# Spreading two norms' inverse roots with two 512-column float32r products each

## The chip, the core and the metric

One core of one Trainium2 chip runs the whole program in one launch. The metric is the device time of an execution in microseconds (us). Three runs of the kernel before took 697.29, 698.58 and 698.46 us; their median is 698.46.

## The reference

A decoder block over 512 positions of width 1024, in fp32:

```python
h  = rmsnorm(x, norm1_g)                       # x * rsqrt(mean(x^2) + eps) * g
P  = h @ w_in                                  # mixer A, q/k/v of mixer B, branch gates, two merge gates
yA = B * causal_dwconv3(C * x_in)
yB = nsa(q, compressed / selected / window keys, gates)
x  = x + W_o(sigmoid(gA) * (yA @ W_A) + sigmoid(gB) * (yB @ W_B))
h  = rmsnorm(x, norm2_g)
x  = x + W_down(silu(causal_dwconv3(W_g h) + b) * (W_u h))   # FFN, inner width 2816

def rmsnorm(x, g):
    x32 = x.astype(jnp.float32)
    y = x32 * lax.rsqrt(jnp.mean(x32 * x32, axis=-1, keepdims=True) + EPS)
    return (y * g.astype(jnp.float32)).astype(x.dtype)
```

Each norm has one inverse root per position, 512 of them.

## The kernel before

Activations are held with channels on the partitions and the 512 positions along the columns. Every large product is made in float32r out of a rounded part and a rest: for a weight tile (wh, wl) and an activation tile (xh, xl), the helper `dense` issues wh·xh, wh·xl and wl·xh (L434, L435, L437), all into one accumulator. Rounded parts are written by ScalarE (ACT), rests by VectorE (DVE), or by a DMA that adds the source to the negated rounded part (L170 to L172).

The norms are not applied to the activations ahead of the products. A product runs on x times its gain, and the inverse root of each position is multiplied in after it. For this the inverse roots, which come out as a 128x4 tile `r` (position on the partition), are needed as a 128x512 tile `rb`: the 512 values along the columns, the same on every partition. `row_scales` makes it: TensorE (PE) sums the squares over the partitions (L400), DVE turns them into means (`ms`, L403), GpSimd (POOL) takes them to the power −0.5 (`r`, L391), PE spreads `r` over the partitions into a PSUM bank `pr`, and ACT copies that to `rb` (L419). The spreading of the first norm (n1) multiplies a tile of ones by the diagonal matrices `dg` (identity times r, made by DVE at L409) in four fp32 products of 128 columns (L412). That of the second (n2) multiplies r, broadcast along the columns, by the identity, in four fp32 products too (L416).

The first norm falls into the token projections (`pj` banks, products at L266 to L268 of `xg_h`, `xg_l` with weights `wh_t`, `wl_t` or `whx`, `wlx`). Its readers are the compressed keys (`kcb`, L469) and later the merge gates. The second falls between the output projection and the FFN.

The FFN works on pairs of 128 inner channels, eleven rounds, by seven products of half-width blocks per pair and matrix (`ff_pair`). The weight forms are `th`/`tl` (one block), `wh_s`/`wl_s` (two blocks, straight from the weights) and `sh`/`sl` (sums of blocks); the activation forms are `xf_h`, `xf_l`; a product has 256 columns. Sums are gathered by DVE in `c` (L1016, L1047), multiplied by `rb`, convolved, put through silu, and multiplied by the second matrix's result. The down projection (`pdn` banks, activations `ah`, `al`, weights `wh_d`, `wl_d`) is worked off between rounds. For the first pair, the first three quarters of the products (L1028) run before the last output projection, to cover the second norm.

Two things set the order of the work. Each engine runs its instructions in one fixed order that a scheduler lays down by simulating the program when it is built. And tiles come from pools: a tile with the same tag as an earlier one waits for that one's last reader. Pools are stacked in SBUF from two sides. On the left lie `sb` (constants, `r`, `rb`), then `pxg` (xg_h, later x1), then `pa` (xg_l, y0, y1, weights of the projections), and after `pa` is closed `px` (xf_h, xf_l) and `pw` (th, tl, sh, sl). On the right lie `pb`, `pp` (with the tag "w4" and whx, wlx), the ring `wf` (its wh and wl serve wh_bo, wh_o, wh_s, wh_d and others) and `pf` (ah, al, c0, c1, cv). Small tiles named `gap_x`, `gap_w` and so on pad the left stack.

Of the kernel before, what the change touches and what calls it, by code (L numbers as in the profile page):

```python
# [11 lines left out]
F32 = mybir.dt.float32  # L12
F32R = mybir.dt.float32r
I32 = mybir.dt.int32
AF = mybir.ActivationFunctionType
ALU = mybir.AluOpType
AX = mybir.AxisListType

P = 128
D = 1024  # L20
S = 512
KD = D // P
NT = S // P
# [19 lines left out]
TOKC = C_G + 24  # L43
NW4 = 4
# [41 lines left out]
def tile_block(ctx: ExitStack, tc: tile.TileContext, xT, pos, par, par2, w_tok, w_a3, w_gate, w_ao, w_bo, w_o,  # L86
               w_ff, w_dn, c_w1, out):
    nc = tc.nc
    sb = ctx.enter_context(tc.tile_pool(name="sb", bufs=1, side="left"))
# [8 lines left out]
    pp = pr_ctx.enter_context(tc.tile_pool(name="pp", bufs=1, side="right"))  # L98

    def const(shape, name, dt=F32, pool=sb):  # L100
        return pool.tile(shape, dt, name=name, tag=name)

    def w_tmp(name, shape):

        t = pp.tile([P, TOKC], F32, name=name, tag="w4", bufs=NW4)
        v = t[:, :math.prod(shape)]
        if len(shape) == 2:
            v = v.rearrange("p (a b) -> p a b", a=shape[0])
        elif len(shape) == 3:
            v = v.rearrange("p (a b c) -> p a b c", a=shape[0], b=shape[1])  # L110
        return v
# [77 lines left out]
    ones = const([P, P], "ones")  # L189
# [90 lines left out]
    sq_sum, first_d = [], []  # L280
# [95 lines left out]
    ident = const([P, P], "ident")  # L376
# [12 lines left out]
    def rsqrt(dst, src, n):  # L389

        nc.gpsimd.tensor_tensor(dst, src, mhalf[:, :n], op=ALU.pow)  # L391
# [3 lines left out]
    def row_scales(total, name, bank_of, dg):  # L395

        pr = bank_of(f"pr_{name}")
        for t in range(NT):
            for i, v in enumerate(total):
                sums = nc.tensor.matmul(pr[:, 2 * t:2 * t + 2], v[:, t * P:(t + 1) * P], ones[:, 0:2],  # L400
                                        start=i == 0, stop=i == len(total) - 1)
        ms = sb.tile([P, NT], F32, name=f"ms_{name}", tag="ms")
        nc.vector.tensor_scalar(ms, pr[:, 0:2 * NT].rearrange("p (t two) -> p t two", two=2)[:, :, 0], 1.0 / D, EPS,  # L403
                                op0=ALU.mult, op1=ALU.add)
        means[name] = ms
        r = sb.tile([P, NT], F32, name=f"r_{name}", tag=f"r_{name}")
        rsqrt(r, ms, NT)
        if dg is not None:
            nc.vector.tensor_tensor(dg, ident[:, None, :].to_broadcast([P, NT, P]), r[:, :, None].to_broadcast([P, NT, P]),  # L409
                                    op=ALU.mult)  # L410
            for t in range(NT):
                rows = nc.tensor.matmul(pr[:, t * P:(t + 1) * P], ones, dg[:, t, :], start=True, stop=True)  # L412
        else:
            for t in range(NT):

                rows = nc.tensor.matmul(pr[:, t * P:(t + 1) * P], r[:, t:t + 1].to_broadcast([P, P]), ident, start=True,  # L416
                                        stop=True)
        rb = sb.tile([P, S], F32, name=f"rb_{name}", tag="rb")
        nc.scalar.activation(rb, pr, AF.Copy)  # L419
        return r, rb, (sums, rows)  # L420

    r1, r1b, _ = row_scales((sq_sum[0][:, 0],), "n1", d_bank, w_tmp("dg_n1", (NT, P)))

    eps1 = const([P, NT], "eps1", F32, pp)
    nc.vector.tensor_scalar(eps1, means["n1"], EPS, None, op0=ALU.mult)
# [25 lines left out]
    for g in range(G):  # L451
        rows = slice((1 - g) * HD, (2 - g) * HD)
# [449 lines left out]
    sq2 = sb.tile([P, S], F32, name="sq2", tag="rb")  # L902
    for n, j in enumerate(O_ORDER):
# [18 lines left out]
        nc.scalar.activation(sq, xj, AF.Square)  # L922
        if n > 0:
            nc.vector.tensor_add(sq2, sq2, sq)
    _, r2b, (sums2, rows2) = row_scales((sq2,), "n2", d_bank, None)
    mx_ctx.close()


    pf = ctx.enter_context(tc.tile_pool(name="pf", bufs=1, side="right"))
# [9 lines left out]

    def pair_tile(name, tag):  # L940
        return pf.tile([P, 2, S], F32, name=name, tag=tag, bufs=1)

    u_bufs = []
    for i in range(NU):
# [106 lines left out]
    def ff_strassen(f, between):  # L1051
        u = u_bufs[f // 2 % NU]

        with tc.high_priority(offset=AHEAD if f == 0 else 0):
            form = ff_forms(f, 0)
        ff_pair(f, 0, u[:, :, 2:], form, late=f == 0 or None)
        between()
        nc.vector.tensor_tensor(u[:, :, 2:], u[:, :, 2:], r2two, op=ALU.mult)
        cv = pair_tile(f"cv{f}", "cv")
        for m in range(2):  # L1060
            conv_silu(f + m, cv[:, m], u[:, m])
        nc.vector.tensor_tensor(cv, cv, r2two, op=ALU.mult)
        up = pair_tile(f"up{f}", "up")
        ff_pair(f, 1, up, ff_forms(f, 1))

        between()
        nc.vector.tensor_tensor(up, up, cv, op=ALU.mult)
        for m in range(2):
            h, l = a_tiles(f + m)
            split(h, l, up[:, m])  # L1070
# [108 lines left out]
```

## Time and profile before

| | |
|---|---|
| runs | 697.29, 698.58, 698.46 us (median 698.46) |
| profiled execution: time, span | 699.54 us, 697.8 us |
| busy: PE, DVE, ACT, POOL | 690.3, 509.2, 436.7, 245.1 us |
| granted TensorE clock | 1.0 (2.4 GHz) over the whole span |
| the spreading of n1, of n2 | starts at 34.31 us, at 373.82 us |
| FFN products of xf with wh_s, wl_s | 363.4 to 660.5 us |

The span goes from the first to the last record of the profiled execution, and all times in the rows count from its start; the execution's own time holds what lies around the span too. A row of a timeline gives the start, the duration, engine, line, operation, tiles and shapes. A matmul's duration contains its whole way through the array and overlaps with the next, so what a product costs is read from one start to the next. An fp32 product leaves two records. A row of the chain of waits gives when a piece began to set the end, for how long, and what it was.

### The profile page before, as it was taken

The numbers are of one execution on the slowest core, as the hardware profiler recorded it, in microseconds if no ns is written. First come the engines' busy times: TensorE is split into PE (matmuls) and PEld (weight loads), VectorE is DVE, ScalarE is ACT, GpSimd is POOL, SyncE is SP. The second block draws the span as 40 slices with busy tenths as digits, with TensorE's granted clock in tenths as the row PEclk, the third lists the DMA queues.
The fourth block names the chain that finished last, engine by engine and source line by source line (L and its number), as shares of the span: only waits on it lengthen the run. The fifth ranks groups of instructions, "written<-read, shape, count | busy, mean of one in ns | idle before, by whom it ended". The sixth has DMA issues, their size and how long they took to land.

```text
span 697.8 us, 11271 instructions
## 1 busy us (share of the span) xinstructions
PE 690.3 (99%) x4123; PEld 615.4 (88%) x4123; DVE 509.2 (73%) x890; ACT 436.7 (63%) x776; POOL 245.1 (35%) x240
## 2 busy tenths in 40 slices
PE   9999999999999999999999999999999999999997
PEld 8999878878888887888889999999999999999986
DVE  6987975766576646376887999888787777877544
ACT  7635754768898877534776776666466665556530
POOL 4151432467888867552012221211112221112110
PEclk9999999999999999999999999999999999999999
DMA  7333686576776555573587977978977979875665
GB/s 264 116 97 121 159 185 142 143 249 203 250 225 214 172 175 151 179 244 100 141 194 169 234 179 190 224 178 200 221 173 173 213 179 213 184 175 108 133 138 151
DMA packets 56615, 124.87 MB, mean 179 GB/s; under 512 B 5232, under 2 KB 20976, under 8 KB 56560
## 3 DMA queue, kind: packets, MB, share of 16 engines
q1 hardware_dynamic: 35648, 79.39, 35.2%
q0 software_dynamic: 13840, 32.51, 27.4%
q10 hardware_dynamic: 7072, 12.26, 5.7%
q8 instruction: 32, 0.52, 0.3%
q14 instruction: 23, 0.19, 0.1%
HBM read 111.55 MB, written 12.58 MB: 178 GB/s over the span
## 4 chain that ended last, share of the span: by engine, by line
PE 87%; DMA 6%; ACT 2%; POOL 2%; issue 1%; DVE 1%; SPq 0%; POOLq 0%; ACTq 0%
PE p L435 10%; PE p L434 10%; PE p L437 10%; PE pdn L435 6%; PE pdn L434 6%; PE pdn L437 6%; PE pg L434 3%; PE pg L435 3%; PE pg L437 3%; DMA tn_e<-td_e 2%; PE po L435 2%; PE po L434 2%; PE po L437 2%; DMA wl_a<-in_w_a_dram 2%; PE pa L437 2%; PE pa L434 2%
## 5 line engine op out<-in xcount | busy, mean ns | idle before, releaser
L434 PE MATMUL p<-xf_h,sh 128*128 128x256 f32 x336 | 80.9, 276 | 0.0
L435 PE MATMUL p<-xf_l,sh 128*128 128x256 f32 x336 | 80.8, 276 | 0.0
L172 POOL DMA_DIRECT2D wl_s<-in_w_ff_dram x22 | 19.4, 883 | 165.4 <-ACT wl_s L171 151.5
L435 PE MATMUL pdn<-al,wh_d 128*128 128x512 f32 (+1 forms) x176 | 68.5, 389 | 0.0
L434 PE MATMUL pdn<-ah,wh_d 128*128 128x512 f32 (+1 forms) x176 | 68.2, 389 | 0.0
L164 ACT ACTIVATE sh<-s 128x1024 fp32r<-128x1024 f32 x44 | 46.4, 1056 | 27.5 <-PE p L435 26.6
L434 PEld LDWEIGHTS p<-xf_h,sh 128*128 128x128 f32 x336 | 63.1, 188 | 0.1
L435 PEld LDWEIGHTS p<-xf_l,sh 128*128 128x128 f32 x336 | 63.1, 188 | 0.1
L165 DVE TENSOR_TENSOR sl<-s,sh 128x1024 fp32r<-128x1024 f32 x44 | 53.5, 1217 | 10.7 <-ACT sh L164 10.7
L170 ACT ACTIVATE wh_s<-wr_s 128x1024 fp32r<-128x1024 f32 x22 | 23.3, 1060 | 57.1 <-PE pdn L435 53.4
L744 POOL TENSOR_TENSOR tn_e<-tn_e,ph 128x512 fp32r<-128x512 f32 x40 | 51.2, 1297 | 16.8 <-ACT ph L743 16.7
L172 POOL DMA_DIRECT2D wl_d<-in_w_dn_dram x22 | 26.4, 1200 | 74.7 <-ACT wl_d L171 73.5
L437 PE MATMUL p<-xf_h,sl 128*128 128x256 f32 x336 | 52.3, 276 | 0.0
L434 PE MATMUL pg<-xg_h,wh_g 128*128 128x512 f32 x128 | 50.2, 392 | 0.0
L435 PE MATMUL pg<-xg_l,wh_g 128*128 128x512 f32 x128 | 50.1, 392 | 0.0
L437 PE MATMUL pdn<-ah,wl_d 128*128 128x512 f32 (+1 forms) x176 | 47.5, 388 | 0.0
L437 PEld LDWEIGHTS p<-xf_h,sl 128*128 128x128 f32 x336 | 44.8, 188 | 0.2
L1098 DVE TENSOR_TENSOR x<-x,pdn 128x512 f32<-128x512 f32 x47 | 32.0, 681 | 16.6 <-PE pdn L437 16.0
L147 POOL TENSOR_TENSOR wl_g<-wr_g,wh_g 128x1024 fp32r<-128x1024 f32 x16 | 38.5, 2407 | 10.3 <-ACT wh_g L145 10.2
L435 PE MATMUL p<-xf_l,wh_s 128*128 128x256 f32 x168 | 40.4, 276 | 0.0
L434 PE MATMUL p<-xf_h,wh_s 128*128 128x256 f32 x168 | 40.4, 277 | 0.0
L437 PEld LDWEIGHTS pdn<-ah,wl_d 128*128 128x128 f32 x176 | 33.0, 188 | 6.8
(367 smaller groups left out, 2096.7 us busy)
## 6 DMA issues: line engine op xcount, KB each, us to landing
wr_s<-in_w_ff_dram SPq DMA_DIRECT2D x44, 512.0 KB, 5.4
wl_s<-in_w_ff_dram POOLq DMA_DIRECT2D x22, 512.0 KB, 7.7
wr_d<-in_w_dn_dram ACTq DMA_DIRECT2D x22, 512.0 KB, 8.0
wl_d<-in_w_dn_dram POOLq DMA_DIRECT2D x22, 512.0 KB, 9.2
wr_g<-in_w_gate_dram SPq DMA_DIRECT2D x16, 512.0 KB, 4.2
wr_a<-in_w_a_dram SPq DMA_DIRECT2D x12, 512.0 KB, 3.8
tl<-in_w_ff_dram POOLq DMA_DIRECT2D x22, 256.0 KB, 7.9
td_e<-e SPq DMA_DIRECT2D x16, 256.0 KB, 4.6
```

The costliest lines, as they stand in the source:

```text
L147: e.tensor_sub(lo[:, 0:n], raw[:, 0:n], hi[:, 0:n].bitcast(F32))
L164: hi = nc.scalar.activation(h, v, AF.Copy)
L165: nc.vector.tensor_sub(l, v, h.bitcast(F32))
L170: nc.scalar.activation(h, raw, AF.Copy)
L172: nc.gpsimd.dma_start(l if dst is None else dst, src, accum_op=ALU.add)
L434: nc.tensor.matmul(acc, wh, xh, start=first and i == 0, stop=False)
L435: nc.tensor.matmul(acc, wh, xl, start=False, stop=False)
L437: nc.tensor.matmul(acc, wl, xh, start=False, stop=last and i == len(units) - 1)
L744: nc.gpsimd.tensor_sub(pl, pt, ph.bitcast(F32))
L1098: nc.vector.tensor_add(xj, xj, acc)
```

## The change

Both norms now split `r` into a rounded part and a rest (`rs`, two instructions of DVE on 128x4), make diagonal matrices of each (two instructions of DVE on 128x512, where n1 had one and n2 none) and multiply ones by them in two float32r products of 512 columns. For n1 the two diagonals lie in a tile of the tag "w4" as before; for n2 they lie in the tag "cv" of `pf`, which is therefore opened ahead of `row_scales`.

```diff
         rsqrt(r, ms, NT)
-        if dg is not None:
-            nc.vector.tensor_tensor(dg, ident[:, None, :].to_broadcast([P, NT, P]), r[:, :, None].to_broadcast([P, NT, P]),
-                                    op=ALU.mult)
-            for t in range(NT):
-                rows = nc.tensor.matmul(pr[:, t * P:(t + 1) * P], ones, dg[:, t, :], start=True, stop=True)
-        else:
-            for t in range(NT):
-
-                rows = nc.tensor.matmul(pr[:, t * P:(t + 1) * P], r[:, t:t + 1].to_broadcast([P, P]), ident, start=True,
-                                        stop=True)
+        rs = sb.tile([P, 2, NT], F32R, name=f"rs_{name}", tag=f"rs_{name}")
+        nc.vector.tensor_copy(rs[:, 0], r)
+        nc.vector.tensor_sub(rs[:, 1], r, rs[:, 0].bitcast(F32))
+        for i in range(2):
+            nc.vector.tensor_tensor(dg[:, i].rearrange("p (t c) -> p t c", t=NT), ident[:, None, :].to_broadcast([P, NT, P]),
+                                    rs[:, i].bitcast(F32)[:, :, None].to_broadcast([P, NT, P]), op=ALU.mult)
+        for i in range(2):
+            rows = nc.tensor.matmul(pr, ones.bitcast(F32R), dg[:, i], start=i == 0, stop=i == 1)
         rb = sb.tile([P, S], F32, name=f"rb_{name}", tag="rb")
...
-    r1, r1b, _ = row_scales((sq_sum[0][:, 0],), "n1", d_bank, w_tmp("dg_n1", (NT, P)))
+    dg1 = pp.tile([P, TOKC], F32R, name="dg_n1", tag="w4", bufs=NW4)[:, 0:2 * S]
+    r1, r1b, _ = row_scales((sq_sum[0][:, 0],), "n1", d_bank, dg1.rearrange("p (i s) -> p i s", i=2))
...
-    _, r2b, (sums2, rows2) = row_scales((sq2,), "n2", d_bank, None)
     mx_ctx.close()
     pf = ctx.enter_context(tc.tile_pool(name="pf", bufs=1, side="right"))
...
+    dg2 = pf.tile([P, 2, S], F32R, name="dg_n2", tag="cv", bufs=1)
+    _, r2b, _ = row_scales((sq2,), "n2", d_bank, dg2)
```

Each `rs` tile takes 32 bytes of every partition in `sb`, so the tiles behind `sb` on the left start 64 bytes further on. The starts that matter, modulo 256 bytes (each step inside these tiles is a multiple of 256):

| tiles | side | start before | start after |
|---|---|---|---|
| xf_h, xf_l, th | left | 32 | 96 |
| sh, sl, tl | left | 224 | 32 |
| xg_h, xg_l, y0, y1, wh_a, wh_g, wh_t | left | 224 | 32 |
| ring: wh_s, wl_s, wh_d, wl_d, wh_o, wh_bo, wl_bo | right | 224 | 224 |
| whx, wlx, ah, al, mix_h, mix_l, qT | right | 224 | 224 |
| kk of head group 0; of head group 1 | right | 96; 224 | 96; 224 |

PE around the spreading of n2, before. `p261_0`, `p11_0` are accumulators of the first FFN round's second matrix, `sh231_0` and `wh_s1_0` weight forms.

```order
L434 MATMUL p261_0_3853<-xf_h_3347,sh231_0_3841 128x256
L416 MATMUL pr_n2_3665<-ident_288,r_n2_3672 128x128 x4
L434 MATMUL p11_0_3852<-xf_h_3347,wh_s1_0_3833 128x256
L435 MATMUL p11_0_3852<-xf_l_3348,wh_s1_0_3833 128x256
L434 MATMUL p11_0_3852<-xf_h_3347,wh_s1_0_3833 128x256
L435 MATMUL p11_0_3852<-xf_l_3348,wh_s1_0_3833 128x256
```

And after, on the same engine and place:

```order
L436 MATMUL p261_0_3859<-xf_h_3349,sl231_0_3848 128x256
L433 MATMUL p11_0_3858<-xf_h_3349,wh_s1_0_3839 128x256
L434 MATMUL p11_0_3858<-xf_l_3350,wh_s1_0_3839 128x256
L415 MATMUL pr_n2_3674<-dg_n2_3673,ones_75 128x512
L433 MATMUL p11_0_3858<-xf_h_3349,wh_s1_0_3839 128x256
L434 MATMUL p11_0_3858<-xf_l_3350,wh_s1_0_3839 128x256
L433 MATMUL p11_0_3858<-xf_h_3349,wh_s1_0_3839 128x256
L434 MATMUL p11_0_3858<-xf_l_3350,wh_s1_0_3839 128x256
L433 MATMUL p11_0_3858<-xf_h_3349,wh_s1_0_3839 128x256
L415 MATMUL pr_n2_3674<-dg_n2_3673,ones_75 128x512
L434 MATMUL p11_0_3858<-xf_l_3350,wh_s1_0_3839 128x256
```

The spreading moved behind the other products of `p261_0` with `sh231_0`, ten products later, and its two products stand apart, with five others between them.

DVE behind the means of n2, before:

```order
L403 TENSOR_SCALAR ms_n2_3670<-pr_n2_3665 128x4
L1016 TENSOR_TENSOR c0_3686<-p260_0_3719,p10_0_3722 128x2x256
L1016 TENSOR_TENSOR c0_3686<-p370_0_3721,c0_3686 128x2x256
L1016 TENSOR_TENSOR c0_3686<-p450_0_3720,c0_3686 128x512
L1047 TENSOR_TENSOR c0_3686<-c0_3686,p450_0_3720 128x256
```

And after:

```order
L403 TENSOR_SCALAR ms_n2_3679<-pr_n2_3674 128x4
L409 CAST rs_n2_3683<-r_n2_3681 128x4
L410 TENSOR_TENSOR rs_n2_3683<-r_n2_3681,rs_n2_3683 128x4
L412 TENSOR_TENSOR dg_n2_3673<-ident_288,rs_n2_3683 128x512 x2
L1017 TENSOR_TENSOR c0_3692<-p260_0_3725,p10_0_3728 128x2x256
```

Four instructions came in ahead of the sums `c0`, and what follows keeps its order.

PE around the spreading of n1, after (before, the four products stood in one row between the second and the third product of `pj_s11`):

```order
L268 MATMUL pj_s11_415<-wl_t11_450,xg_h_95 128x384
L415 MATMUL pr_n1_306<-dg_n1_305,ones_75 128x512
L266 MATMUL pj_s12_416<-wh_t11_449,xg_h_95 128x384
L267 MATMUL pj_s12_416<-wh_t11_449,xg_l_96 128x384
L268 MATMUL pj_s12_416<-wl_t11_450,xg_h_95 128x384
L266 MATMUL pj_o1_417<-wh_t11_449,xg_h_95 128x384
L267 MATMUL pj_o1_417<-wh_t11_449,xg_l_96 128x384
L415 MATMUL pr_n1_306<-dg_n1_305,ones_75 128x512
```

The two products stand one and seven rows further back than the block did. In the eleven rounds of the FFN the scheduler's order of PE, DVE and ACT differs by a few rows here and there; the order of the SP and POOL queues is the same.

## The prediction

> **What bounds the kernel now.** I read the page's head first, then the chain, then TensorE's waits.
>
> ```profile
> span 697.8 us, 11271 instructions
> PE 690.3 (99%) x4123; PEld 615.4 (88%) x4123; DVE 509.2 (73%) x890; ACT 436.7 (63%) x776; POOL 245.1 (35%) x240
> PEclk9999999999999999999999999999999999999999
> PE 87%; DMA 6%; ACT 2%; POOL 2%; issue 1%; DVE 1%; SPq 0%; POOLq 0%; ACTq 0%
> ```
>
> TensorE (PE) is busy for 690.3 of 697.8 us, its granted clock stays at the upper level (2.4 GHz) in all 40 slices, and the chain that ended last runs on it for 87%. The only waits of PE on a producer in mid-kernel are these two, 2.7 us in all:
>
> ```profile
> PE po L746 <- ACT ph L743: 1.8, 2, 1.4
> PE pa L437 <- DMA wl_a<-in_w_a_dram: 0.9, 1, 0.9
> ```
>
> So what the change does to PE's stream is what it does to the time, as long as no producer falls behind. The profiled execution took 699.54 us, 1.74 more than its span and 1.08 above the median of the runs shown (698.46); the sum below is a difference, taken against that profile, and I add it to the median.
>
> **The products taken out and put in.** The four fp32 products of the first norm appear as eight records.
>
> ```profile
> 34.13 0.34 PE L267 MATMUL pj_s<-wh_t,xg_l 128*128 128x384 f32 x1
> 34.31 1.05 PE L412 MATMUL pr_n<-dg_n,ones 128*128 128x128 f32 x8
> 35.12 0.42 PE L268 MATMUL pj_s<-wl_t,xg_h 128*128 128x384 f32 x1
> 35.37 0.33 PE L266 MATMUL pj_s<-wh_t,xg_h 128*128 128x384 f32 x1
> ```
>
> From 34.13 to 35.37 lie the block and two 384-column products. Such a product ahead of the block takes 34.31 − 34.13 = 0.18 us, the one behind it 0.25, so the block costs 1.24 − 2 × 0.175 = 0.89 us. The chain gives the second norm's block the same price:
>
> ```profile
> 373.99 0.89 PE pr_n L416 x8
> 374.88 0.12 PE p L434
> ```
>
> In their place stand two float32r products of 512 columns each. The nearest price is that of the kernel's own 512-column products, from one start to the next:
>
> ```profile
> 443.89 0.39 PE L434 MATMUL pdn<-ah,wh_d 128*128 128x512 f32 x1
> ...
> 445.48 0.39 PE L435 MATMUL pdn<-al,wh_d 128*128 128x512 f32 x1
> ```
>
> Seven starts later is 1.59 us later: 0.227 us each, 0.45 for two. Per norm 0.89 − 0.45 = 0.44 us is saved, over both norms 0.88. Both ends: at the 0.25 us that a disturbed product took above, the saving is 0.78; at 0.227 it is 0.88. I take 0.88, −0.13% of the time.
>
> The Trainium skill ("FP8 and Floating Point Precision", "TensorE Precision Notes") says that true fp32 needs four passes through the array; worked out from it, an estimate is that four products of 128 columns cost as much as four of 512, so 8 × 0.227 = 1.8 us would go and the saving would be 0.9 per norm. The trace shows half of that, two records per product, and the rows above decide.
>
> **What VectorE gets in exchange.** Per norm a copy and a subtraction on 128x4, and one (first norm) or two (second norm) more products of 128x512.
>
> ```profile
> 29.62 0.69 DVE L409 TENSOR_TENSOR dg_n<-ident,r_n 128x512 f32<-128x512 f32 x1 [0.86 <-POOL r_n L391]
> 30.23 0.16 DVE L427 TENSOR_SCALAR r1h<-r_n 128x4 f32<-128x4 f32 x1
> 49.34 0.56 DVE L596 TENSOR_TENSOR t<-t,qst 128x384 f32<-128x384 f32 x1 [0.56 <-POOL qst L391]
> 52.52 1.80 DVE L469 TENSOR_TENSOR kcb<-pkc,rb_n 64x256 f32<-64x256 f32 x3 [2.62 <-PE pkc L437]
> ```
>
> A 128x512 product holds DVE for 0.61 us (29.62 to 30.23), a 128x4 instruction for at most 0.16. The first norm adds 0.61 + 2 × 0.16, some 0.9 us. Behind it DVE works without a gap until the 0.56 us before 49.34 and the 2.62 us before 52.52, where it waits for PE: the delay ends there, and PE waits for nothing in that stretch. If that slack were gone, up to 0.3 us would reach PE through the split halves that DVE makes for the products behind 50 us; I take zero. dg was written by 30.3 and pr started at 34.31; DVE is 0.9 us later with it, so PE doesn't wait there either. Bound: 0 to +0.3.
>
> ```profile
> 369.79 0.15 DVE L403 TENSOR_SCALAR ms_n<-pr_n 128x4 f32<-128x4 f32 x1
> 372.49 0.69 DVE L1016 TENSOR_TENSOR c<-p,p 128x512 f32<-128x512 f32 x1 [2.55 <-ACT p L1038]
> 375.27 2.36 DVE L165 TENSOR_TENSOR sl<-s,sh 128x1024 fp32r<-128x1024 f32 x2 [0.17 <-ACT sh L164]
> ```
>
> The second norm adds 2 × 0.61 + 2 × 0.16 = 1.5 us, all between the r of GpSimd and c at 372.49. DVE is idle for 2.55 us there, of which 1.1 are spent until r is ready:
>
> ```profile
> 370.03 1.03 POOL L391 TENSOR_TENSOR r_n<-ms_n,mhalf 128x4 f32<-128x4 f32 x1
> 377.13 0.58 ACT L419 ACTIVATE rb_n<-pr_n 128x512 f32<-128x512 f32 x1
> ```
>
> 371.06 + 1.5 = 372.6: c starts 0.1 us late, and the 0.17 us of idle time before 375.27 takes that in. Cost zero; if the idle time were gone, 0.1. ScalarE comes to its copy of rb in its own order only at 377.13, whereas the second pr product now stands 15 products of 0.12 us behind the place of the old block (373.82), so it ends near 376: nothing waits longer for rb. No DMA and no GpSimd instruction is added or moved past another; the SP and POOL queues keep their order.
>
> **What moves without being named.** The two rs tiles take 2 × 32 bytes of each partition in the pool of constants, which lies ahead of every other tile on the left of SBUF. All of those move by 64 bytes; what lies on the right doesn't (the table of starts is in the section on the change). Now the trace: products of 256 columns in the same stage, with the same xf, take two different times.
>
> ```profile
> 446.77 0.12 PE p L434
> ...
> 447.72 0.45 PE p L437 x4
> 448.18 0.11 PE p L434
> ...
> 449.08 0.45 PE p L437 x4
> ```
>
> The eight pieces from 446.77 to 447.72 are products of xf with th: 0.95 / 8 = 0.119 us. Then come tl (0.45 / 4 = 0.1125) and wh_s (448.18 to 449.08, 0.90 / 8 = 0.1125). By the layout th starts in the same place within 128 bytes as xf, tl and wh_s 64 bytes off. The same holds in another stage, with 512 columns: four products of kk whose place differs from qT's by 128 bytes modulo 256 take 0.92 us (119.28 to 120.20), 0.230 each, against the 0.227 of ah and wh_d above, which start in equal places.
>
> ```profile
> 119.28 0.39 PE L659 MATMUL sc<-kk,qT 128*128 128x512 f32 x1
> ...
> 120.20 0.39 PE L434 MATMUL pa<-xg_h,wh_a 128*128 128x512 f32 x1
> ```
>
> After the change xf lies 128 bytes from wh_s and wl_s modulo 256, so they get the relation that kk has there. It concerns 504 products:
>
> ```profile
> L435 PE MATMUL p<-xf_l,wh_s 128*128 128x256 f32 x168 | 40.4, 276 | 0.0
> L434 PE MATMUL p<-xf_h,wh_s 128*128 128x256 f32 x168 | 40.4, 277 | 0.0
> L437 PE MATMUL p<-xf_h,wl_s 128*128 128x256 f32 x168 | 26.1, 276 | 0.0
> ```
>
> ```profile
> 204.44 0.28 PE L659 MATMUL sc<-kk,qT 128*128 128x256 f32 x1
> ...
> 204.67 0.39 PE L435 MATMUL pg<-xg_l,wh_g 128*128 128x512 f32 x1
> ```
>
> The mean of the 504 from start to start is 114.1 ns over the whole trace (first at 363.4, last at 660.5 us). At th's 118.8 they would cost 504 × 4.7 = +2.4 us; at the 117.4 of the eight 256-column kk products that have that relation (the two below are the first, 0.23 us for the pair), +1.7. Below it the bound is 0, if place is not the cause. I take +2.2, nearer th, which is of the same size, operand and stage.
>
> Three smaller terms. (a) The relation of y and wh_bo in the 96 pmb products changes from equal to 64 bytes off; no row shows 512 columns so. Bounds by kk's 0.230 and, for twice the loss of th, 0.236, against 0.227: 0 to +0.9; I take +0.3, since 256 columns in that relation run at the best rate seen. (b) The 120 products of xg with whx and wlx change in the same way; at 4 ns either way, −0.5 to +0.5; zero. (c) The sh and sl products keep their relation, but run slower for a while after other work:
>
> ```profile
> 421.87 0.47 PE p L437 x4
> ```
>
> 0.1175 us each, behind a block of pdn, where tl above took 0.1125; in the trace some 290 products of the left-side halves and wh_s run so, until a run of th ends it. With wh_s like th, such phases may end sooner: 0 to −0.6 us (146 products of 4.5 ns); I take −0.3.
>
> Sum: −0.88 + 2.2 + 0.3 − 0.3 = **+1.3 us**, 698.46 + 1.3 = 699.8. About 0.2% (1.4 us) is what a measurement of this kernel can tell from no change, so the forecast lies just at that edge.
>
> **The rivals.**
>
> *Place doesn't matter.* Then th is slower for another reason (what stands before it, say), only the products count, and the time is 698.46 − 0.88 = 697.6: no change that can be told. For it speaks that 512-column products of ah and wh_d in equal places run at 0.227, twice 0.1135, without any loss. Against it speaks that th is slow in every one of its runs (84 with xf_h, 84 with xf_l). The Trainium skill holds with this rival: "SBUF — State Buffer", section "Who interferes with whom", gives PE two independent read ports, one for the moving operand and one for the weights, and says "PE and ACT never wait on anyone." By that rule the time is this rival's 697.6; th beside tl and wh_s in the rows above doesn't agree with it.
>
> *Place is neutral and the slow phases shrink.* The new order near 374 us has no fp32 block, behind which wh_s went on at 0.12 (the row at 374.88). If the 290 slow products all went back to 0.113, 290 × 4.5 ns = 1.3 us more would go: 698.46 − 0.88 − 1.3 = 696.3, faster. It decides only if fp32 or place was what kept those phases up; the row at 421.87 shows one behind plain pdn, against it.
>
> *The slow phase spreads.* wh_s and wl_s are the rests between runs of sh and sl. If products in the new relation don't end the phase but start it, the 1,056 products of sh and sl go from 114.1 to 117.8: +3.9 us on top, 698.46 + 1.3 + 3.9 = 703.7. For it: 128 bytes is not quite th's relation of 0; against it: th ends such phases.
>
> *The reordered FFN makes PE wait.* The scheduler moves products and split halves in the eleven rounds of the FFN by a few rows. The longest wait that PE has on such a producer is the 1.4 us above; one of that kind gives 699.0 without a penalty of place (−0.88 + 1.4), 701.2 with it.
>
> **How the numbers follow.** The forecast 0.48, split evenly at the edge of 1.4 us; place neutral 0.24; slow phases shrink 0.09; the phase spreads 0.09; a new wait 0.10. Faster by over 0.2%: 0.09 and a little of the neutral case's spread, 0.12. Within 0.2%: half of the forecast, nearly all of the neutral case, a third of the waits, 0.46. Slower: 0.42. The range reaches from 696.8 (the neutral case with half of the slow phases gone) to 702.0 (th's price in full, pmb's in full, and half a wait), and leaves out about 2 in 10. The forecast's own range is 699.0 to 700.8.
>
> **What would show it.** In the profile after: the pr rows as two products of 0.23 us; no new wait of PE at 34 or 374; rb copied by ScalarE near 377; wh_s pieces of the chain at 0.12 instead of 0.11, and the xf, wh_s mean at 117 to 119 ns from start to start; th unchanged at 0.12; pmb at 0.227 or above. The prediction is wrong if wh_s stays at 0.1125 with xf 128 bytes off, or if sh and sl change their rate though they keep their relation.

## The result, and the profile after

The changed kernel takes 704.75 us (median; 704.03 to 705.11) against 698.46 before: the ratio is 1.009, with a 95% interval of 1.0079 to 1.0102. It is slower by 6.3 us; the prediction gave 699.8 and a range that ended at 702.0. The head of its page:

```profile
span 703.0 us, 11250 instructions
PE 697.2 (99%) x4111; PEld 622.3 (89%) x4111; DVE 512.0 (73%) x897; ACT 436.9 (62%) x776; POOL 241.8 (34%) x240
PEclk9999999999999999999999999999999999999999
PE 93%; DMA 3%; POOL 2%; issue 1%; DVE 1%; ACT 1%; POOLq 0%; ACTq 0%
```

PE is busy for 697.2 us, 6.9 more than before, with 12 records fewer and at the same granted clock. The other engines' busy times hardly moved. PE's waits in mid-kernel became shorter, 1.1 us in all against 2.7:

```profile
PE pa L436 <- DMA wl_a<-in_w_a_dram: 0.7, 1, 0.7
PE po L745 <- ACT ph L742: 0.4, 1, 0.4
```

So nothing new is waited for: the products themselves take longer. The products that were changed do not. The timeline of PE at the first norm and at the second:

```profile
34.67 0.39 PE L415 MATMUL pr_n<-dg_n,ones 128*128 128x512 f32 x1
34.90 0.34 PE L266 MATMUL pj_s<-wh_t,xg_h 128*128 128x384 f32 x1
...
373.95 0.40 PE L415 MATMUL pr_n<-dg_n,ones 128*128 128x512 f32 x1
374.18 0.28 PE L433 MATMUL p<-xf_h,wh_s 128*128 128x256 f32 x1
```

Each takes 0.23 us to the next start, 0.93 for the four (231, 231, 235 and 230 ns), where eight fp32 products had taken 1.78 with the delay of the product behind each block.

The loss is in the FFN. Here is the chain of waits in the round of which the prediction showed the end of th and the start of wh_s; each piece of four is one group of products with a rest, in the order tl, wl_s, wl_s, sl, sl:

```profile
446.40 0.12 PE p L433
...
447.36 0.46 PE p L436 x4
...
448.76 0.48 PE p L436 x4
...
450.18 0.47 PE p L436 x4
...
451.60 0.47 PE p L436 x4
...
453.01 0.47 PE p L436 x4
```

Only tl, right behind th, is near the old 0.45; wl_s and sl are at 0.47 to 0.48. Before, the second wl_s and both sl of that round stood at 0.45 as well:

```profile
450.44 0.45 PE p L437 x4
...
451.80 0.45 PE p L437 x4
...
453.16 0.45 PE p L437 x4
```

The intervals from one start to the next, averaged over the whole trace (intervals above 400 ns, which hold waits, left out), show where it went:

| products | number | before, ns | after, ns | difference, us |
|---|---|---|---|---|
| sh, sl | 1056 | 114.2 | 117.8 | +3.9 |
| wh_s, wl_s | 528 | 114.2 | 118.3 | +2.2 |
| th, tl | 264 | 117.5 | 118.6 | +0.3 |
| wh_d, wl_d (512 columns) | 522 | 227.7 | 228.3 | +0.3 |
| wh_bo, wl_bo | 96 | 226.7 | 229.8 | +0.3 |
| pr | 16 records, now 4 | 100.9 | 231.8 | −0.7 |

That is +6.3 us. It is as much as the medians differ by, but the two traces themselves are only 5.2 us apart (spans 703.0 and 697.8): the intervals above 400 ns sum to 2.0 us less after the change, and other products take 0.9 more. The largest term belongs to products whose two tiles moved together. Of the 1,056 products of sh and sl, 865 took under 115.6 ns before; after the change it is one.

### The profile page after: what moved, and what is told of

Its sections match the earlier page's. It is cut to its first block, busy times and chain, and to the rows that moved or that the text cites. A ratio compares the mean times of both kernels' runs of the same rounds, so it can differ in the third digit from the quotient of the medians.

```text
span 703.0 us, 11250 instructions
## 1 busy us (share of the span) xinstructions
PE 697.2 (99%) x4111; PEld 622.3 (89%) x4111; DVE 512.0 (73%) x897; ACT 436.9 (62%) x776; POOL 241.8 (34%) x240
## 4 chain that ended last, share of the span: by engine, by line
PE 93%; DMA 3%; POOL 2%; issue 1%; DVE 1%; ACT 1%; POOLq 0%; ACTq 0%
PE p L434 10%; PE p L433 10%; PE p L436 10%; PE pdn L434 6%; PE pdn L433 6%; PE pdn L436 6%; PE pg L433 4%; PE pg L434 4%; PE pg L436 4%; PE pa L436 2%; PE pa L433 2%; PE pa L434 2%; PE po L433 2%; PE po L434 2%; PE po L436 2%; DMA wl_a<-in_w_a_dram 2%
## 5 line engine op out<-in xcount | busy, mean ns | idle before, releaser
L434 PE MATMUL p<-xf_l,sh 128*128 128x256 f32 x336 | 82.9, 280 | 0.0
L433 PE MATMUL p<-xf_h,sh 128*128 128x256 f32 x336 | 82.9, 280 | 0.0
L434 PE MATMUL p<-xf_l,wh_s 128*128 128x256 f32 x168 | 42.0, 281 | 0.0
L172 POOL DMA_DIRECT2D tl<-in_w_ff_dram x22 | 19.4, 881 | 59.1 <-ACT tl L171 52.5
```

The costliest lines, as they stand in the source:

```text
L172: nc.gpsimd.dma_start(l if dst is None else dst, src, accum_op=ALU.add)
L433: nc.tensor.matmul(acc, wh, xh, start=first and i == 0, stop=False)
L434: nc.tensor.matmul(acc, wh, xl, start=False, stop=False)
```

## The experiments

Theory P: the place of xf against wh_s and wl_s costs their products directly and leaves a slow phase in which sh and sl run too. Rival O: the changed order, or the missing fp32 block, does it. Each kernel was timed against the kernel before on the same chip; that one's median was 698.3 to 698.7 us in these sets.

**The change without its 64 bytes** (a_place). The two rs tiles get free columns of tiles that are there anyway.

```diff
-    def row_scales(total, name, bank_of, dg):
+    def row_scales(total, name, bank_of, dg, rs):
...
-        rs = sb.tile([P, 2, NT], F32R, name=f"rs_{name}", tag=f"rs_{name}")
...
-    _, r2b, _ = row_scales((sq2,), "n2", d_bank, dg2)
+    _, r2b, _ = row_scales((sq2,), "n2", d_bank, dg2, pf.tile([P, 2, S], F32R, name="rs_n2", tag="up", bufs=1)[:, :, 0:NT])
```

The first norm is handed `dg1[:, 2 * S:2 * S + 2 * NT]` of its "w4" tile in the same way.

> The changed kernel with the two rs tiles laid into free columns of tiles that exist already (the dg tile of the first norm, the tag up for the second), so that nothing on the left of SBUF moves. Theory P (the place of xf against wh_s and wl_s costs their 504 products directly and also keeps sh and sl slow): the four fp32 products are saved and nothing else happens, 698.46 - 0.88 = 697.6 us; sh and sl back at 114 ns. Rival O (the changed order, or the missing fp32 block, keeps the slow phase up): 704.7, as the changed kernel.

697.53 us, ratio 0.9993 (0.9983 to 1.0003). The whole loss is gone. PE's order is that of the changed kernel, but for the two products of n1, which stand a few rows further back. sh and sl are at 114.0 ns, wh_s and wl_s at 114.4. The chain in the same round, the groups tl, wl_s, wl_s, sl:

```profile
447.38 0.45 PE p L436 x4
...
448.74 0.45 PE p L436 x4
...
450.10 0.45 PE p L436 x4
...
451.46 0.45 PE p L436 x4
```

**The 64 bytes without the change** (b_pad64), in the kernel before:

```diff
-    warm = const([P, 2], "warm")
+    warm = const([P, 2], "warm"); const([P, 16], "gap_s")
```

> The kernel before with 64 unused bytes more in the pool of constants, no instruction changed. Theory P: what the changed kernel lost, without its saving: 704.75 + 0.88 = 705.6 us, sh and sl at 118 ns, wh_s and wl_s at 118.3. Rival O: 698.5.

705.36 us, ratio 1.0105 (1.0087 to 1.0123); of four executions three took 704.58 to 705.40 us and one 2609, on which nothing here rests. No instruction differs from the kernel before, and the loss is complete:

```profile
447.89 0.46 PE p L437 x4
...
449.29 0.48 PE p L437 x4
...
450.72 0.47 PE p L437 x4
...
452.13 0.47 PE p L437 x4
```

With these two, rival O falls. By the rule of the Trainium skill that the prediction weighed ("SBUF — State Buffer", "Who interferes with whom": PE never waits on anyone for SBUF), an unused tile would cost nothing, as the prediction read it; it cost 7 us here. No run shows whether it is for SBUF that PE waits.

**Only the FFN's tiles put back** (a_gapx): in the changed kernel, 192 bytes more in gap_x ahead of xf.

```diff
-    const([P, 80], "gap_x", F32, px)
+    const([P, 128], "gap_x", F32, px)
```

> The changed kernel with 192 bytes more of padding ahead of xf, so that xf, th, tl, sh and sl come back to their old starts modulo 256, while everything of the earlier stages stays 64 bytes off. Theory P in its narrow form (only the FFN's relations count): 697.6 + 0.3 for pmb = 697.9 us. Rival (the projections' and the gates' places cost as well): up to 2 us above that. Rival O: 704.7.

698.25 us, ratio 1.0008 (0.9995 to 1.0021): the earlier stages' new places cost next to nothing. Seen of them are pmb's 229.8 ns against 226.7, and 229.8 against 229.1 in the 384 products of wh_g and wl_g, 0.3 us each.

**128 bytes in place of 64** (a_gap128): the same line with 96, so that the FFN's left tiles lie 128 bytes up.

> The changed kernel with 64 bytes more of padding ahead of xf, so that xf, th, tl, sh and sl lie 128 bytes above their old starts, not 64. Theory P (the difference to wh_s and wl_s modulo 128 counts, 64 is the fast one): as a_gapx, 697.9 us (up to 698.3), with sh, sl, wh_s and wl_s at 114 ns. Rival (the fast place is one modulo 256, or a place of its own): 701 to 704.7.

698.91 us, ratio 1.0001 (0.9988 to 1.0014); sh and sl 113.8, wh_s and wl_s 114.2. Twice the shift costs nothing.

**Ring and left tiles moved, the relation kept** (b_both): the kernel before, with xf and the FFN's left tiles 64 bytes up, the ring and the pools below it 64 bytes down.

```diff
-    const([P, 80], "gap_x", F32, px)
+    const([P, 96], "gap_x", F32, px)
...
-    TH = S // 2
+    TH = S // 2; const([P, 16], "gap_r", F32, wf)
```

> The kernel before with xf, th, tl, sh and sl 64 bytes up and the ring with ah, al, c and cv 64 bytes down, so that xf again lies 64 bytes modulo 128 from wh_s and wl_s. Theory P (the relation counts): 698.5 to 698.9 us (pmb gets the relation it has in the changed kernel). Rival A (the place of sh, sl or xf itself counts, whatever the ring does): sh and sl stay at 118 ns, 702.4 us or more.

698.46 us, ratio 1.0007 (0.9998 to 1.0015), though xf, sh and sl start exactly where they do in the changed kernel. Rival A falls too: what counts is xf against the ring.

**The ring in equal places** (a_ring0): a_place with gap_x at 128, so that the difference of xf to wh_s is 0, as for th, and not 128.

> The kernel a_place with xf, th, tl, sh and sl moved so that xf starts at the same place as wh_s and wl_s modulo 256 (difference 0, as th has, in place of 128). Theory P3 (0 and 128 differ: 0 ends the slow phase, as th does): wh_s and wl_s at 118.8, sh and sl at 114, 697.5 + 2.4 = 699.9 us. Theory P4 (only the place modulo 128 counts): as the changed kernel without its move of y, sh and sl at 118, 703.5 to 704.5 us.

701.31 us, ratio 1.0048 (1.0031 to 1.0064). The chain of one round, in the order tl, wl_s, wl_s, sl:

```profile
447.79 0.46 PE p L436 x4
...
449.21 0.48 PE p L436 x4
...
450.65 0.48 PE p L436 x4
...
452.04 0.45 PE p L436 x4
```

wh_s and wl_s pay, 120.2 ns on average, but sh and sl come back to 113.8. P3 is right in kind, 1.4 us too low in its time: with 256 columns, equal places cost only the products that have them, while a difference of 128, in the changed kernel, also costs those that come after.

**th at 128 bytes** (a_th128): a_place with th alone moved by 128 bytes (a pad of 128 bytes ahead of it, gap_w cut to 64).

> The kernel a_place with th alone moved by 128 bytes, so that it stands to xf as wh_s and wl_s do in the changed kernel. Theory P3 (a difference of 0 ends the slow phase, one of 128 doesn't): wh_s, wl_s, sh and sl at 117 to 118 as in a_thopp, 702.5 to 703.5 us. Rival P4 (both equal modulo 128, both end it): 697.5.

704.05 us, ratio 1.0072 (1.0058 to 1.0086). P4 falls; P3's range ended 0.5 us lower. The groups tl and wl_s behind th are slow now, though their own places are as before:

```profile
447.29 0.47 PE p L436 x4
...
448.70 0.47 PE p L436 x4
```

**th 64 bytes off** (a_thopp): no 256-column product has equal places (pad 64, gap_w 128).

> The kernel a_place with th moved by 64 bytes too, so that no 256-column product has equal places. Theory P1 (th is what ends the slow phase behind every block of pdn): sh, sl, wh_s and wl_s stay at 117.8, 697.5 + (1056 + 528) x 3.7 ns = 703.4 us. Rival (equal places are only a loss): th falls to 113, 697.5 - 176 x 5.5 ns = 696.5 us.

703.09 us, ratio 1.0068 (1.0055 to 1.0082). sh and sl 117.1, wh_s and wl_s 117.2, as P1 had it: without a run of products in equal places between the blocks of pdn and the rest, the slow phase stays. In the round at 446 us, tl and wl_s:

```profile
446.20 0.47 PE p L436 x4
...
447.61 0.47 PE p L436 x4
```

**All of it 64 bytes off** (a_opp): a_thopp with ah, al, mix_h and mix_l moved against the ring as well.

```diff
-    wf = ctx.enter_context(tc.tile_pool(name="wf", bufs=1, side="right"))
+    wf = ctx.enter_context(tc.tile_pool(name="wf", bufs=1, side="right")); const([P, 16], "gap_r", F32, wf)
```

> The kernel a_thopp with ah, al, mix_h and mix_l moved by 64 bytes as well, so that from the output projection on no product has equal places. Theory P5 (the slow phase is started by the 512-column products in equal places, whose first products after a switch take 230 to 236 ns): no phase starts, 697.5 - 1.0 (th) - 1.3 (slow phases) - 0.5 (pdn) = 694.7 us. Rival P6 (the phase is there from earlier and only a run in equal places ends it): all of the 256-column products at 117.8 and the 512-column ones at 231, 703.4 + 2.5 = 706 us.

700.86 us, ratio 1.0039 (1.0022 to 1.0056). Neither P5 nor P6 as written: all 256-column products are fast (sh, sl 113.9, wh_s, wl_s 114.0, th 113.9), as P5 had it, but the 512-column ones of pdn and po went from 227.9 and 228.4 (in a_place) to 233.2 ns, some 3.7 us over their 714. P5 did not see that. One product of pdn, tl and wl_s of a round:

```profile
443.98 0.24 PE pdn L433
...
447.69 0.45 PE p L436 x4
...
449.05 0.45 PE p L436 x4
```

Where 256 columns like a difference of 64, 512 columns like 0. The order of PE's products is that of a_thopp, and only the 512-column products changed their relation; so it was these, in equal places, that left the slow phase behind in a_thopp.

**th behind wh_s** (a_thlast): the changed kernel, with the products of `a22` (th) issued behind those of `a11` and `a12` (wh_s).

> The changed kernel with the products of xf with th and tl issued behind those with wh_s and wl_s in every round, not ahead of them; no tile moves. Theory P1 (a run of wh_s and wl_s in the new relation leaves the slow phase up, a run of th ends it): sh and sl behind th go back to 113 to 114 ns and give back most of the 3.9 us, 701 us (700.5 to 702); wh_s and wl_s stay at 118. Rival P2 (the slow phase of sh and sl comes from their share in the stream or from the later blocks, whatever stands ahead): 704.7.

703.92 us, ratio 1.0082 (1.0069 to 1.0095). P1 as stated missed by 3 us. In the round at 447 us it holds, the first group below being wl_s, the second tl and the third sl:

```profile
447.36 0.48 PE p L436 x4
...
448.79 0.45 PE p L436 x4
...
450.15 0.45 PE p L436 x4
```

That round is the last of its kind. Of the 20 full runs of th, the six up to there end the phase (tl behind them at 113 to 114 ns), and the 14 from 463 us on do not (118); 201 of the 1,056 products of sh and sl are under 115.6 ns. So a run of th behind wh_s and wl_s at a difference of 128 does not always end the phase, and no run here says what decides.

**Half way** (a_gap32): a_place with gap_x at 88, so that the difference of xf to the ring is 96 modulo 128.

> The kernel a_place with xf, th, tl, sh and sl 32 bytes up, so that xf lies 96 bytes modulo 128 from wh_s and wl_s, half way between the fast and the slow relation. Theory G (a clash of equal 64-byte pieces; a difference of 96 clashes only in part): between 697.5 and 701, wh_s and wl_s at 115 to 118 ns. Theory E (only starts that agree modulo 128 clash): as a_place, 697.5. Rival (only 64 is free): as the changed kernel, 703.5 to 704.5.

701.49 us, ratio 1.0041 (1.0027 to 1.0055). wh_s and wl_s take 119.7 ns, somewhat more than at a difference of 128; sh and sl, at 114.5, hardly suffer. Theory E is wrong: the starts need not agree modulo 128 to clash. Theory G missed too: the time is just above its upper end, and 119.7 is no part of the price but all of it (a_ring0's equal places: 120.2).

The relations and the means of the traces, in ns (the difference is xf minus the tile, modulo 256):

| kernel | time, us | xf − wh_s | xf − th | wh_s, wl_s | sh, sl |
|---|---|---|---|---|---|
| before | 698.46 | 64 | 0 | 114.2 | 114.2 |
| changed | 704.75 | 128 | 0 | 118.3 | 117.8 |
| a_place | 697.53 | 64 | 0 | 114.4 | 114.0 |
| a_gap128, b_both | 698.91, 698.46 | 192 | 0 | 114.2, 114.1 | 113.8, 114.2 |
| a_ring0 | 701.31 | 0 | 0 | 120.2 | 113.8 |
| a_gap32 | 701.49 | 96 | 0 | 119.7 | 114.5 |
| a_gapx | 698.25 | 64 | 0 | 114.0 | 114.0 |
| a_thlast (th behind wh_s) | 703.92 | 128 | 0 | 119.5 | 116.9 |
| a_opp (512-column products moved too) | 700.86 | 64 | 192 | 114.0 | 113.9 |
| a_thopp | 703.09 | 64 | 192 | 117.2 | 117.1 |
| a_th128 | 704.05 | 64 | 128 | 117.7 | 117.6 |

## Why the prediction was wrong

*The bound* was right: PE sets the time, and no new wait came.

*The products* were right: 0.88 us less was forecast, 0.85 is seen (1.78 against 0.93). In the time it is less certain, since a_place's interval reaches from −1.2 to +0.2 us. The sentence on four passes was worked out wrongly: four products of 128 columns, four passes each, are as many columns as four products of 512, by estimate 4 × 0.227 = 0.91 us a norm, which leaves a saving of 0.45 a norm, not 0.9; the trace has 0.89 for the block. The Trainium skill ("FP8 and Floating Point Precision", "TensorE Precision Notes") and the trace agree there.

*VectorE* was right in its cost, though the 0.56 us of idle time before 49.34 are a wait for GpSimd (qst), as the row says, not for PE. The timeline of DVE and of ACT at the second norm:

```profile
370.27 1.29 DVE L412 TENSOR_TENSOR dg_n<-ident,rs_n 128x512 fp32r<-128x512 f32 x2
371.47 0.68 DVE L1017 TENSOR_TENSOR c<-p,p 128x512 f32<-128x512 f32 x1
...
376.07 0.58 ACT L417 ACTIVATE rb_n<-pr_n 128x512 f32<-128x512 f32 x1
```

Both products took 1.2 us, c began right behind them, and ACT came to rb only after the second pr product (374.78 to 375.01).

*Place* was right as a cause and, for wh_s and wl_s, in size: +2.2 forecast, +2.2 seen. So was pmb, +0.3 each. The size of wh_s and wl_s is in part luck: in a_th128 they kept their old relation and took 117.7 ns from the slow phase alone, against 118.3 in the changed kernel, so the seen 2.2 us can't be put down to their own places only.

*Term (c) failed,* the slow phase of sh and sl. It took the products at a difference of 128 to be like th and to end the slow phase of sh and sl: −0.3 us. They do the opposite, and the term measured +3.9. The prediction had this as the rival in which the phase spreads, at 703.7 us; its price was right to a tenth, its chance of 0.09 was not, and the range left it out. The step behind it was to lump differences of 0 and 128 together as equal modulo 128, although its own rows with 512 columns told them apart: kk at 128 took 0.230, ah and wh_d at 0 took 0.227. a_ring0 and a_th128 tell the two apart: at 0 the products behind are fast, at 128 they are not. Another 0.6 us lie in th, tl and pdn, which no term held.

*The range's ends* were added up wrongly as well: its own terms give 696.9 (697.6 − 0.65) and 701.6 (698.46 − 0.88 + 2.4 + 0.9 + 0.7), not 696.8 and 702.0. Neither reaches what was measured.

What stays open is the cause inside the engine. The traces show that the rate of a product depends on the places of its tiles and on the products before it, not what keeps that memory; and a_thlast shows that the rule "equal places end the slow phase" has exceptions which no run here explains.

## What to carry to other kernels

When PE is busy all the time, a tile of a few bytes can cost more than the instructions that were saved: look at what a new allocation moves, and put small tiles where nothing stands behind them, or pad so that the starts behind come back to what they were modulo 256 bytes, as a_gapx did. In a_gap128 a shift of 128 cost nothing either, but the same shift of th alone cost 6.5 us (a_th128 against a_place). The version with the small tiles put elsewhere (a_place) keeps the change without its loss; it can't be told from the kernel before, and is 1% faster than the changed one. And where a rate depends on what ran before, a product's price in the trace holds only for its neighbours there: ask what the products behind it will take, not only what it takes.

## What was not expected of the hardware

A stream of 256-column float32r products can run at 113.3 or at 117.8 ns for hundreds of products on end, with the same tiles, clock and order; 64 unused bytes ahead of xf, sh and sl decide which (sh, sl: 865 of 1,056 fast before, 21 with the pad alone). A difference of 32 bytes from the fast place cost the products that had it 5 ns (119.7 against 114.4). And with 512 columns it is the equal places that are faster: pdn took 227.9 ns so, and 233.2 at a difference of 64.
